# A two-layer trunk on one core: the state-space stage without GpSimd arithmetic, and the first fetched rows moved in the first expert stage

## The chip, the cores and the metric

The kernel runs on one core of one Trainium2 chip. Its time is device microseconds (us). Before the change three runs gave 1828.47, 1831.72 and 1833.39 us; the median is 1831.72 us. The profile is of one further execution of 1835.46 us, whose span from the first to the last instruction is 1833.7 us.

The names of the engines in the profile: PE is TensorE's matmul, PEld its weight load, DVE is VectorE, ACT is ScalarE, POOL is GpSimd, SP is SyncE, which here only sends for data. A q behind a name (SPq, POOLq) is that engine's own queue of semaphore waits and DMA issues.

## The reference

256 image tokens and 256 context tokens of 1024 channels go through two layers, all in float32. Layer 0 mixes tokens by attention and by a state-space scan (SSD), layer 1 by two kinds of attention. After each mixer stand a residual with a layer norm and a mixture of 32 experts. What the change touches:

```python
# the state-space branch: a depthwise convolution of 5 taps, then silu
u = jax.nn.silu(depthwise_conv_centred(xbc, conv_w, conv_b))
xs, bm, cm = split(u)                       # 1024 + 512 + 512 channels
# ssd_chunk_scan, per chunk of 128 tokens, 4 groups of 4 heads, two directions
decay = exp(where(lower, a_cs[l] - a_cs[s], -inf))
y_diag = einsum(decay * (cm @ bm.T), x)
y_off  = einsum(cm, h_in, exp(a_cs))
# the experts: each token goes to 2 of 32
x   = layer_norm(ALPHA * x + gate * mix, ln_g[0], ln_b[0])
f   = hier_moe(modulate(x, ...))            # w2[e] (silu(w1[e] x) * (w3[e] x))
out = layer_norm(ALPHA * x + gate5 * f, ln_g[1], ln_b[1])
```

## The kernel before, in words

The work runs in stages: the first modulation and the attention of layer 0 (up to about 240 us of the trace), the state-space scan (240 to 480 us), the output projection, residual and routing (to 580 us), the experts of layer 0 (to about 1095 us), then the same for layer 1. Apart from instructions that the code pins (`mmp`, `trp` and a few more), the order on each engine is set when the program is built, by a scheduler that weighs costs; at run time each engine works its list strictly in that order.

**The state-space scan** (`ssd0`) goes through 4 groups. For each group three units of the input projection are split into a high and a low part (`split`, L99 on ACT and L100 on DVE or POOL: `wh`, `wl`), and PE multiplies in three passes (L105 to L107, `pfm`). `self.lo_pool` says which half of a unit has its low part made on POOL. `ssd_conv` then convolves: ACT copies the projection out of PSUM into a padded buffer (`up`, L643), DVE makes the first tap and the bias with one TENSOR_SCALAR (L646), and the four other taps with SCALAR_TENSOR_TENSOR (L648, `acc`). There are 4 groups of 4 such blocks. `ssd_group` takes the decay rows `bc` from DRAM, per chunk `t`: `ce = exp(bc)` on ACT (L796) times `cT` on POOL (L797; 512 columns for the chunks 0 and 1, 1024 for 2 and 3), the difference of the decays by 4 SCALAR_TENSOR_TENSOR on DVE (L802), and twice the product with the mask `cbm` (L808): direction 1 on POOL, direction 0 on DVE. PE sums the products into `py` (L815).

**The experts of layer 0** (`moe`, `nt == 4`) stream weights: each expert needs 6 transfers of 1 MB (L430), into a ring of 12 buffers. A transfer is issued by SP when PE has used the buffer's last contents. For expert `e`, `expert_up` makes the product with w1 and w3 in two halves (`a`, 16 matmuls each), `expert_turn` turns the gated result of the expert before it (`hp`), `expert_down` multiplies by w2 (`py`). Experts come in groups of 4 that share a gathered input `xg`. The input of group 0 comes by matmul. For group 1 and later, POOL fetches the token rows from DRAM by an indirect DMA (`fetch`, L1126), by a row number that PE and DVE make in `group_gates` (`pgs`, then `ix`, L1125), and PE turns them in four steps (`turn_rows`, 4 transposes each, L201 `pg`). `steps` is the list of such pending pieces, and `fill(n, steps)` does n of them at a place in the loop over experts. Since PE's order is pinned there, all later matmuls stand behind a transpose that waits for its rows.

Between expert 0 and the loop stands the residual's affine part: POOL multiplies the 4 tiles of the residual `S` by `ALPHA * ln_g` and adds `ALPHA * ln_b` (L1043, 16 instructions; ACT scales the rows first, L1041). Its constant `alpha` is made from `odest`, so that it starts after the routing.

Of the kernel before, what the change touches and what calls it, by code (L numbers as in the profile page):

```python
# [24 lines left out]
F32 = mybir.dt.float32  # L25
# [3 lines left out]
AF = mybir.ActivationFunctionType  # L29
OP = mybir.AluOpType  # L30
# [4 lines left out]
ALPHA = 4.0 ** 0.25  # L35
# [32 lines left out]
class Trunk:  # L68
# [5 lines left out]
    def pool(self, name, side="left"):  # L74
# [3 lines left out]
        a="rkb pfm pv pck pgk pcq pgq pmq pmv pmk a13 pna pout1",  # L78
# [249 lines left out]
    def mixer0(self):  # L328
        nc, tc, I = self.nc, self.tc, self.I
# [61 lines left out]
            qk = [self.fm(self.w_in(0), hTh, hTl), self.fm(self.w_in(1), hTh, hTl, "pfm2")]  # L391
        self.late_consts()
        self.attention0(qk, small, hTh, hTl, naT, dtb, ad)
        self.lo_pool = lambda jh: jh % 2
        self.ssd0(small, hTh, hTl, YT, dtb, ad, es_a)
        es_h.close()
        self.moep = self.left.enter_context(self.pool("moe"))
# [236 lines left out]
    def ssd_conv(self, sp, g, hTh, hTl, YT, cw, cb, dsk, ups):  # L634
        nc, I, V = self.nc, self.I, self.nc.vector
        bT = sp.tile([128, 512], F32, name="bT", bufs=2)
        cT = sp.tile([128, 512], F32, name="cT", bufs=2)
        xs = sp.tile([128, 4, 256], F32, name="xs", bufs=2)
        Bt = sp.tile([128, 4, 128], F32, name="Bt", bufs=2)

        def sink(f, p):
            up = ups[f % 2]
            nc.scalar.activation(up[:, :, 2:258], p.rearrange("p (s n) -> p s n", s=2), AF.Copy)  # L643
            acc = sp.tile([128, 2, 256], F32, name="acc", bufs=2)
            k = 4 * g + f
            V.tensor_scalar(acc, up[:, :, 0:256], cw[:, k, 0:1], cb[:, k:k + 1], op0=OP.mult, op1=OP.add)  # L646
            for i in range(1, 5):
                V.scalar_tensor_tensor(acc, up[:, :, i:i + 256], cw[:, k, i:i + 1], acc, op0=OP.mult, op1=OP.add)  # L648
            th = sp.tile([128, 2, 256], F32, name="th", bufs=1)
            nc.scalar.activation(th, acc, AF.Tanh)  # L650
            dst = th if f < 2 else (bT if f == 2 else cT).rearrange("p (s n) -> p s n", s=2)
            V.scalar_tensor_tensor(dst, th, 1.0, acc, op0=OP.add, op1=OP.mult)
            if f < 2:
                dfl = dst.rearrange("p s n -> p (s n)")
                nc.scalar.activation(YT[:, 2 * g + f, :], dfl, AF.Copy, scale=dsk[:, 2 * g + f:2 * g + f + 1])
            if f < 3:
                dfl = dfl if f < 2 else bT
                pt = self.ps([128, 4, 128], "xsT")
                for t in range(4):
                    self.tr(pt[:, t], dfl[:, t * 128:(t + 1) * 128])  # L660
                nc.scalar.activation(xs[:, :, f * 128:(f + 1) * 128] if f < 2 else Bt, pt, AF.Copy)

        for u in range(2):
            self.proj_fm(self.w_in(6 + 2 * g + u), hTh, hTl, lambda f, p, u=u: sink(2 * u + f, p))
        return bT, cT, xs, Bt
# [80 lines left out]
    def ssd_group(self, sp, g, bT, cT, xs, Bt, YT, masks, dd):  # L746
# [40 lines left out]
        for t in range(4):  # L787
            sl = slice(t * 128, (t + 1) * 128)
            bc = sp.tile([128, 2, 4, 128], F32, name="bc", bufs=3)
            src = atd[t, :, 4 * g:4 * g + 4, :]  # L790
            nc.sync.dma_start(bc, bass.AP(tensor=src.tensor, offset=src.offset,
                                          ap=[[0, 128], [2048, 2], [128, 4], [1, 128]]))
            dirs = {0: (1,), 1: (0,), 2: (0, 1), 3: (0, 1)}[t]
            d0, d1 = dirs[0], dirs[-1] + 1
            ce = sp.tile([128, 2, 4, 128], F32, name="ce", bufs=2)
            nc.scalar.activation(ce[:, d0:d1], bc[:, d0:d1], AF.Exp)  # L796
            nc.gpsimd.tensor_tensor(ce[:, d0:d1].rearrange("p d r l -> p (d r) l"), ce[:, d0:d1].rearrange("p d r l -> p (d r) l"),  # L797
                            cT[:, None, sl].to_broadcast([128, 4 * (d1 - d0), 128]), OP.mult)
            for r in range(4):
                h = 4 * g + r  # L800
                nc.scalar.activation(bc[:, 1, r], bc[:, 1, r], AF.Identity, bias=nacs[:, t, 16 + h:17 + h])
                V.scalar_tensor_tensor(bc[:, 0, r], bc[:, 0, r], acs[:, t, h:h + 1], bc[:, 1, r],  # L802
                                       op0=OP.subtract, op1=OP.min)
            nc.scalar.activation(bc[:, 0], bc[:, 0], AF.Exp)

            M = bc
            for d in (1, 0):
                (nc.gpsimd if d else V).tensor_tensor(M[:, d], bc[:, 0],  # L808
                                                      cbm[d][:, t:t + 1, :].to_broadcast([128, 4, 128]), OP.mult)
            for f in range(2):  # L810
                terms = [(xdt[d][:, t, :], M[:, d]) for d in range(2)] + [(hst[d][t][:, 0], ce[:, d]) for d in dirs]
                for i, (l, m) in enumerate(terms):
                    for s in range(2):
                        r = 2 * f + s
                        nc.tensor.matmul(py[f][64 * s:64 * s + 64, t, :], l[:, r * 64:(r + 1) * 64], m[:, r],  # L815
                                         start=(i == 0), stop=(i == len(terms) - 1))
# [171 lines left out]
    def moe(self, layer, tiles):  # L988
# [4 lines left out]
        with ExitStack() as es:  # L993
            with self.pool("exp", "right") as ep:
# [5 lines left out]
                def fill(n, q=todo):  # L1000
                    for _ in range(min(n, len(q))):
                        q.pop(0)()
# [27 lines left out]
                fill(2, steps)  # L1030
                self.expert_up(cur, 0, 1)
                self.route_rest(nt)

                alpha = ep.tile([128, 1], F32, name="alpha")
                V.tensor_scalar(alpha, self.odest[:, nt - 1, 1:2], 0.0, ALPHA, op0=OP.mult, op1=OP.add)
                for h in range(2):
                    k = slice(512 * h, 512 * h + 512)
                    for n, y, op in (('ln_g', "yh", OP.mult), ('ln_b', "yl", OP.add)):
                        a = ep.tile([128, 512], F32, name=y, bufs=3)
                        nc.gpsimd.dma_start(a, self.bcast(I[n][layer, 0, k], 512))  # L1040
                        nc.scalar.activation(a, a, AF.Copy, scale=alpha)  # L1041
                        for t in tiles:
                            G.tensor_tensor(S[:, t, k], S[:, t, k], a, op)  # L1043
                self.dump(f'L{layer}_dest', self.dest)
                self.dump(f'L{layer}_gate', self.gate)
                prev = None
# [4 lines left out]
                for e in range(nb + 1):  # L1051
# [5 lines left out]
                    if cur and e:  # L1057
                        self.expert_up(cur, 0)
                    fill(2)
                    fill(2 if e > 28 or nt == 4 and e % 4 == 1 else 1, steps)  # L1060
                    if prev:
                        self.expert_turn(prev)
                    if cur:
# [17 lines left out]
                    if e == 0:  # L1081
                        group(1)
                        fill(2 if nt == 2 else 1, steps)
                    if e % 4 == 3 and e < 27:
                        group(e // 4 + 2)
                    if e == 27:
# [78 lines left out]
    def group_gates(self, ep, nt, oh, e, rows=None):  # L1165

        gs = ep.tile([64, 4], F32, name="gs", bufs=3)
        for i in range(2):
# [2 lines left out]
                self.mmp(pg.rearrange("p a b -> p (a b)"), oh[:, t, 128 * i:128 * i + 128], self.gdr[:, t].rearrange("p a b -> p (a b)"),  # L1171
                         start=(t == 0), stop=(t == nt - 1))
            if rows is not None:
                self.fetch(ep, rows[:, i], pg[:, 0, 32:33])
            for k in range(2):
                self.nc.vector.tensor_reduce(gs[:, 2 * i + k:2 * i + k + 1], pg[64 * k:64 * k + 64, :, e + 2 * i + k], AX.X, OP.add)
        return gs
# [770 lines left out]
```

## Time and profile before

| what | value |
|---|---|
| runs (us) | 1828.47, 1831.72, 1833.39; median 1831.72 |
| profiled execution (us) | 1835.46, span 1833.7 |
| PE, DVE, ACT, POOL busy (us) | 1680.1, 968.9, 507.8, 374.6 |
| mean granted TensorE clock | 0.953 of full speed |
| DMA | 536.16 MB, mean 292 GB/s |

The busy times are averages over stages that differ: in the two expert stages the DMA engines are busy all the time at 420 GB/s, and in the stages between them at a half or less. A stage has to be read on its own.

### The profile page before, as it was taken

What the parts mean: (1) busy time and instruction counts of PE and PEld (TensorE: products, weight loads), DVE (VectorE), ACT (ScalarE), POOL (GpSimd) and SP (SyncE); (2) the same over time, 40 slices, a digit from 0 to 9 for tenths busy, and PEclk for the clock granted to TensorE, in tenths of its full rate; (3) what the DMA queues carried; (4) which work ended last, traced back from release to release, by engine and by line L of the source; (5) the groups of instructions that cost most, each with busy time, mean ns of one, the idle gap of its engine ahead of it and who ended that gap; (6) DMA issues with size and microseconds to landing.
All of it is one profiled execution on the core that took longest, in us unless ns stands there. A gap on an engine that the chain in (4) does not pass through costs nothing. (4 is left out here: it accounts for less than half of the span.)

```text
span 1833.7 us, 21779 instructions
## 1 busy us (share of the span) xinstructions
PE 1680.1 (92%) x8093; PEld 871.2 (48%) x8093; DVE 968.9 (53%) x2025; ACT 507.8 (28%) x987; POOL 374.6 (20%) x313
## 2 busy tenths in 40 slices
PE   7999989999898799999999995989979999999995
PEld 2665646557455343444443333856444444444441
DVE  2454469878667155544554447774553333433325
ACT  2423434434122111111111113467321111111111
POOL 2211114433122322121211114331020000100101
PEclk8999999999998899999999996989989999999997
DMA  9665265654626799999999971253369999999993
GB/s 340 212 205 186 77 227 172 223 197 114 235 76 241 310 419 420 421 421 420 421 421 420 413 325 62 79 218 114 123 256 421 421 421 421 421 420 421 421 420 143
DMA packets 103072, 536.16 MB, mean 292 GB/s; under 512 B 20657, under 2 KB 24753, under 8 KB 49329
## 3 DMA queue, kind: packets, MB, share of 16 engines
q1 hardware_dynamic: 98032, 519.69, 71.9%
q0 software_dynamic: 4928, 15.02, 2.3%
q8 instruction: 66, 1.08, 0.2%
q14 instruction: 46, 0.37, 0.1%
HBM read 531.36 MB, written 3.30 MB: 292 GB/s over the span
## 5 line engine op out<-in xcount | busy, mean ns | idle before, releaser
L197 PE MATMUL a<-ringw,xg 128*64 128x512 f32 x1584 | 371.4, 611 | 0.8 <-DVE ovbase L1833 0.5
L197 PEld LDWEIGHTS a<-ringw,xg 128*64 128x64 f32 x1584 | 114.4, 141 | 212.8 <-issue 205.7
L1196 DVE TENSOR_TENSOR ym<-pcm,mod 128x512 f32<-128x512 f32 x136 | 90.6, 688 | 168.5 <-PE pcm L197 167.5
L1773 DVE TENSOR_TENSOR yl<-py,yh 64x512 fp32r<-64x512 f32 x130 | 89.5, 688 | 162.5 <-ACT yh L1772 162.4
L1197 POOL TENSOR_TENSOR S<-S,ym 128x512 f32<-128x512 f32 x68 | 86.5, 1272 | 403.7 <-DVE ym L1196 403.7
L1772 ACT ACTIVATE yh<-py 64x512 fp32r<-64x512 f32 x130 | 76.9, 591 | 275.1 <-PE py L197 224.3
L197 PE MATMUL py<-ringw,g 128*64 128x512 f32 x640 | 146.0, 597 | 0.0
L1197 POOL TENSOR_TENSOR S<-S,two 128x512 f32<-128x512 f32 x32 | 40.9, 1278 | 410.3 <-DVE two L1196 410.3
L197 PE MATMUL a<-raw,xg 128*64 128x512 f32 x496 | 116.2, 607 | 1.8 <-DMA raw<-in_moe_w_dram 1.8
L105 PE MATMUL pfm<-hTh,wh 128*128 128x512 f32 x256 | 107.5, 421 | 8.5 <-ACT up L643 5.8
L216 PE MATMUL adaps<-adw,cs 128*32 128x512 f32 x384 | 97.6, 656 | 13.5 <-DMA adw<-in_ada_w_dram 13.4
L100 POOL TENSOR_TENSOR wl<-raw,wh 128x512 fp32r<-128x512 f32 (+1 forms) x46 | 58.7, 1281 | 237.2 <-ACT wh L99 148.0
L106 PE MATMUL pfm<-hTh,wl 128*128 128x512 f32 x256 | 104.5, 408 | 0.0
L107 PE MATMUL pfm<-hTl,wh 128*128 128x512 f32 x256 | 101.5, 403 | 0.0
L1747 ACT ACTIVATE sa<-a 64x512 f32<-64x512 f32 x65 | 38.4, 591 | 217.0 <-PE a L197 217.0
L197 PE MATMUL pcm<-yh,ohT 128*128 128x512 f32 (+1 forms) x200 | 91.6, 458 | 6.6 <-DVE ym L1196 4.5
L1196 DVE TENSOR_TENSOR two<-pcm,S 128x512 f32<-128x512 f32 x64 | 42.7, 689 | 94.7 <-PE pcm L197 94.2
L197 PE MATMUL py<-raw,g 128*64 128x512 f32 x400 | 91.3, 598 | 0.5 <-ACT g L1756 0.5
L197 PEld LDWEIGHTS py<-ringw,g 128*64 128x64 f32 x640 | 43.8, 136 | 81.1 <-issue 74.1
L197 PE MATMUL pcm<-yl,ohT 128*128 128x512 f32 (+1 forms) x200 | 81.1, 406 | 0.6 <-DVE yl L1773 0.6
L197 PEld LDWEIGHTS pcm<-yh,ohT 128*128 128x128 f32 (+1 forms) x200 | 38.2, 191 | 91.4 <-issue 64.8
L1748 DVE SCALAR_TENSOR_TENSOR sa<-sa,gs,a 64x512 f32<-64x512 f32 x64 | 47.9, 749 | 52.0 <-ACT sa L1747 50.6
(519 smaller groups left out, 2872.8 us busy)
## 6 DMA issues: line engine op xcount, KB each, us to landing
ringw<-in_moe_w_dram SPq DMA_DIRECT2D x278, 1024.0 KB, 16.5
raw<-in_moe_w_dram SPq DMA_DIRECT2D x112, 1024.0 KB, 15.2
adw<-in_ada_w_dram SPq DMA_DIRECT2D x96, 512.0 KB, 5.2
raw<-in_w_in_dram SPq DMA_DIRECT2D x18, 1024.0 KB, 6.9
bc<-atd SPq DMA_DIRECT2D x16, 512.0 KB, 6.6
raw<-in_w_out_dram SPq DMA_DIRECT2D x4, 1024.0 KB, 5.9
raw<-in_o_w_out_dram SPq DMA_DIRECT2D x4, 1024.0 KB, 4.8
bias<-in_rpb_dram SPq DMA_DIRECT2D x8, 256.0 KB, 4.8
```

Of the source, the lines that this page charges most:

```text
L100: (eng or nc.vector).tensor_tensor(lo, src, hi, OP.subtract)
L105: mm(out, ah, bh, start=start, stop=False)
L106: mm(out, al, bh, start=False, stop=False)
L107: mm(out, ah, bl, start=False, stop=stop)
L197: return self.tc.keep_in_program_order(self.nc.tensor.matmul(*args, **kw))
L216: self.nc.tensor.matmul(p[32 * g:32 * g + 32, :], self.cs[:, j, :], w[:, (g - g0) * 512:(g - g0 + 1) * 512], start=(j == 0), stop=(j == 7))
L1196: nc.vector.tensor_tensor(m, p, self.rows5[t // 2][:, k], OP.mult)
L1197: (nc.gpsimd if i % 2 == 0 else nc.vector).tensor_tensor(S[:, t, k], S[:, t, k], m, OP.add)
L1747: self.nc.scalar.activation(s, a[0:64, :], AF.Silu)
L1748: self.nc.vector.scalar_tensor_tensor(s, s, E['gs'], a[64:128, :], op0=OP.mult, op1=OP.mult)
L1772: nc.scalar.activation(c[h][0][r], py[q], AF.Copy)
L1773: V.tensor_tensor(c[h][1][r], py[q], c[h][0][r], OP.subtract)
```

## The change

Four edits of the state-space stage and two of the expert stage:

1. `lo_pool` is False there: all low parts `wl` of the stage's projections are made on DVE.
2. The middle tap and the bias are made by ACT, straight from PSUM (ACTIVATE Identity with scale and bias); DVE adds the other four taps. The TENSOR_SCALAR is gone.
3. `ce` times `cT` is on DVE.
4. Both products with `cbm` are on DVE.
5. The affine part of layer 0 is issued after the fetch of group 1's rows, and `alpha` is made from that fetch's row number; for layer 1 (`nt == 2`) it stays.
6. The turning of group 1's rows, formerly two steps at expert 1 and one each at experts 2 and 3, is now two at expert 2 and two at expert 3.

```diff
-        self.lo_pool = lambda jh: jh % 2
+        self.lo_pool = lambda jh: False
...
-            nc.scalar.activation(up[:, :, 2:258], p.rearrange("p (s n) -> p s n", s=2), AF.Copy)
...
-            V.tensor_scalar(acc, up[:, :, 0:256], cw[:, k, 0:1], cb[:, k:k + 1], op0=OP.mult, op1=OP.add)
-            for i in range(1, 5):
+            pv = p.rearrange("p (s n) -> p s n", s=2)
+            nc.scalar.activation(up[:, :, 2:258], pv, AF.Copy)
+
+            nc.scalar.activation(acc, pv, AF.Identity, scale=cw[:, k, 2:3], bias=cb[:, k:k + 1])
+            for i in (0, 1, 3, 4):
                 V.scalar_tensor_tensor(acc, up[:, :, i:i + 256], cw[:, k, i:i + 1], acc, op0=OP.mult, op1=OP.add)
...
-            nc.gpsimd.tensor_tensor(ce[:, d0:d1].rearrange("p d r l -> p (d r) l"), ce[:, d0:d1].rearrange("p d r l -> p (d r) l"),
+            V.tensor_tensor(ce[:, d0:d1].rearrange("p d r l -> p (d r) l"), ce[:, d0:d1].rearrange("p d r l -> p (d r) l"),
...
-                (nc.gpsimd if d else V).tensor_tensor(M[:, d], bc[:, 0],
+                V.tensor_tensor(M[:, d], bc[:, 0],
...
+                if nt == 2:
+                    affine(self.odest[:, nt - 1, 1:2])
...
-                    fill(2 if e > 28 or nt == 4 and e % 4 == 1 else 1, steps)
+
+                    fill({1: 0, 2: 2, 3: 2}.get(e, 2 if e > 28 or e % 4 == 1 else 1) if nt == 4 else 2 if e > 28 else 1, steps)
...
                         fill(2 if nt == 2 else 1, steps)
+                        if nt == 4:
+                            affine(self.number)
...
-                self.fetch(ep, rows[:, i], pg[:, 0, 32:33])
+                self.number = pg[:, 0, 32:33]
+                self.fetch(ep, rows[:, i], self.number)
```

POOL at the start of the expert stage, before (`rows` are the fetched rows, `S` the residual, `yh` and `yl` the scaled rows of ln_g and ln_b):

```order
L1040 DMA yl<-in_ln_b_dram 128x512
L1043 TENSOR_TENSOR S<-S,yh 128x512 x4
L1126 DMA rows<-h2d,ix 128x1024
L1043 TENSOR_TENSOR S<-S,yh 128x512 x2
L1043 TENSOR_TENSOR S<-S,yl 128x512
L1043 TENSOR_TENSOR S<-S,yh 128x512 x2
L1126 DMA rows<-h2d,ix 128x1024
L1043 TENSOR_TENSOR S<-S,yl 128x512 x7
```

And the same place of the changed program (L1126 has become L1135, L1043 is L1046):

```order
L1043 DMA yl<-in_ln_b_dram 128x512
L1135 DMA rows<-h2d,ix 128x1024 x2
L1046 TENSOR_TENSOR S<-S,yh 128x512 x7
L1046 TENSOR_TENSOR S<-S,yl 128x512
L1046 TENSOR_TENSOR S<-S,yh 128x512
L1046 TENSOR_TENSOR S<-S,yl 128x512 x7
```

Both fetches now stand ahead of all 16 affine instructions, where the second one stood behind nine. PE in the same place, before, from the row numbers (`pgs`) on:

```order
L197 MATMUL pgs<-gdr,two_4502 128x66 x8
L197 MATMUL a_4540<-ringw,xg 64x512 x8
L201 MATMUL pg<-ident,rows 128x128 x8
L201 MATMUL hp<-ident,sa 128x64 x4
L197 MATMUL a_4540<-raw,xg 64x512 x8
L201 MATMUL poT<-ident,two_4180 128x128 x4
```

And of the changed program:

```order
L197 MATMUL pgs<-gdr,two_4472 128x66 x8
L197 MATMUL a_4540<-ringw,xg 64x512 x8
L201 MATMUL hp<-ident,sa 128x64 x4
L197 MATMUL a_4540<-raw,xg 64x512 x8
L201 MATMUL poT<-ident,two_4180 128x128 x4
L197 MATMUL py_4582<-raw,g 64x512 x8
L197 MATMUL a_4603<-ringw,xg 64x512 x8
L201 MATMUL pg<-ident,rows 128x128 x8
L201 MATMUL hp<-ident,sa 128x64 x4
```

The first eight transposes of the rows have moved behind the rest of expert 1 and the first half of expert 2. The last chunks of the last group on DVE, before (`cb` are the masked products, `YT` the result):

```order
L784 TENSOR_TENSOR h_3505<-h_3505,pst 128x256
L802 SCALAR_TENSOR_TENSOR bc<-bc,acs 128x128 x8
L808 TENSOR_TENSOR bc<-bc,cb_3467 128x512 x2
L819 TENSOR_TENSOR YT<-YT,py 128x512
L679 SCALAR_TENSOR_TENSOR YT<-zt,YT 128x512
```

And of the changed program:

```order
L786 TENSOR_TENSOR h_3505<-h_3505,pst 128x256
L799 TENSOR_TENSOR ce<-ce,cT 128x1024
L804 SCALAR_TENSOR_TENSOR bc<-bc,acs 128x128 x4
L799 TENSOR_TENSOR ce<-ce,cT 128x1024
L804 SCALAR_TENSOR_TENSOR bc<-bc,acs 128x128 x2
L810 TENSOR_TENSOR bc<-bc,cb_3468 128x512
L804 SCALAR_TENSOR_TENSOR bc<-bc,acs 128x128 x2
L810 TENSOR_TENSOR bc<-bc,cb_3467 128x512
L810 TENSOR_TENSOR bc<-bc,cb_3468 128x512
L810 TENSOR_TENSOR bc<-bc,cb_3467 128x512
L821 TENSOR_TENSOR YT<-YT,py 128x512
```

What POOL did for these two chunks (two `ce`, two products) now stands in DVE's own list, between its other work.

## Rows read from the trace of the kernel before

**Rows 1.** Busy time by stage: stretch, length, engines' busy us, clock, DMA share, GB/s
```profile
240.00:480.00 240.00, 219.85 (x1226) 145.81 (x1228) 195.39 (x293) 99.00 (x195) 88.81 (x62) 0.94 0.54 175
...
598.90:617.10 18.20, 7.49 (x31) 3.53 (x30) 0.69 (x1) 0.98 (x2) 13.94 (x12) 0.72 0.48 176
617.10:1075.00 457.90, 440.84 (x2024) 185.32 (x2026) 225.06 (x385) 82.54 (x151) 86.78 (x70) 0.98 1.01 418
```

**Rows 2.** The same in 10 us slices, one slice of the state-space stage
```profile
330.00:340.00 10.00, 9.28 (x36) 5.99 (x36) 10.00 (x17) 4.42 (x7) 4.09 (x1) 0.83 0.60 214
```

**Rows 3.** POOL's groups, 240 to 480 us: count, busy us, mean ns, idle before
```profile
L808 POOL TENSOR_TENSOR bc<-bc,cb 128x512 f32<-128x512 f32 x16 | 28.4, 1781 | 19.3 <-issue 7.2 <-ACT bc L804 6.6 <-DVE cb L762 5.4
L100 POOL TENSOR_TENSOR wl<-raw,wh 128x512 fp32r<-128x512 f32 x16 | 21.9, 1370 | 82.5 <-ACT wh L99 41.2 <-DVE acc L648 29.6 <-issue 11.0
L797 POOL TENSOR_TENSOR ce<-ce,cT 128x1024 f32<-128x1024 f32 x8 | 19.1, 2396 | 23.4 <-ACT ce L796 23.4
L797 POOL TENSOR_TENSOR ce<-ce,cT 128x512 f32<-128x512 f32 x8 | 12.2, 1525 | 28.2 <-DVE cT L652 13.0 <-ACT ce L796 5.6 <-ACT bc L801 4.4
```

**Rows 4.** DVE's groups, 240 to 480 us
```profile
L648 DVE SCALAR_TENSOR_TENSOR acc<-up,cw,acc 128x512 f32<-128x512 f32 x56 | 49.4, 890 | 0.5
L802 DVE SCALAR_TENSOR_TENSOR bc<-bc,acs 128x128 f32<-128x128 f32 x64 | 48.1, 787 | 5.8 <-ACT bc L801 5.8
L646 DVE TENSOR_SCALAR acc<-up,cw,cb 128x512 f32<-128x512 f32 x14 | 12.5, 896 | 2.9 <-ACT up L643 2.6
```

**Rows 5.** Single lines on DVE: ns shortest/median/longest, first and last start
```profile
L802 DVE SCALAR_TENSOR_TENSOR bc<-bc,acs x64: 335/345/3331, 244.1 to 476.7; 128x128 f32<-128x128 f32 x64
...
L648 DVE SCALAR_TENSOR_TENSOR acc<-up,cw,acc x56: 734/745/1878, 244.9 to 431.0; 128x512 f32<-128x512 f32 x56
...
L646 DVE TENSOR_SCALAR acc<-up,cw,cb x14: 530/547/1601, 243.7 to 421.6; 128x512 f32<-128x512 f32 x14
...
L808 DVE TENSOR_TENSOR bc<-bc,cb x16: 672/680/1754, 282.0 to 479.1; 128x512 f32<-128x512 f32 x16
...
L767 DVE TENSOR_TENSOR xdt<-xs,dt x8: 1210/1219/2320, 260.4 to 439.6; 128x1024 f32<-128x1024 f32 x8
```

**Rows 6.** Order of time, POOL and DVE at 300 us: start us, us
```profile
300.29 2.41 POOL L797 TENSOR_TENSOR ce<-ce,cT 128x1024 f32<-128x1024 f32 x1
...
300.65 2.20 DVE L802 SCALAR_TENSOR_TENSOR bc<-bc,acs 128x128 f32<-128x128 f32 x1
```

**Rows 7.** Order of time, DVE at the end of the state-space stage
```profile
469.06 4.99 DVE L802 SCALAR_TENSOR_TENSOR bc<-bc,acs 128x128 f32<-128x128 f32 x4 [0.81 <-ACT bc L801]
```

**Rows 8.** Order of time, TensorE at experts 0 and 1 [idle before]
```profile
593.11 5.80 PE L197 MATMUL a<-ringw,xg 128*64 128x512 f32 x16
601.67 0.38 PE L201 MATMUL pg<-ident,rows 128*128 128x128 f32 x1 [2.76 <-DMA rows<-h2d,ix]
610.00 1.76 PE L201 MATMUL pg<-ident,rows 128*128 128x128 f32 x7 [7.95 <-DMA rows<-h2d,ix]
```

**Rows 9.** Order of time, DVE: the row numbers
```profile
591.61 0.16 DVE L1125 CAST ix<-pgs 128x1 int32<-128x1 f32 x1 [0.54 <-PE pgs L197]
...
593.22 0.16 DVE L1125 CAST ix<-pgs 128x1 int32<-128x1 f32 x1 [1.22 <-PE pgs L197]
```

**Rows 10.** Order of time, POOL: the two fetches
```profile
596.03 1.05 POOL L1126 DMA_INDIRECT rows<-h2d,ix  x1 [0.16 <-issue]
...
603.41 1.01 POOL L1126 DMA_INDIRECT rows<-h2d,ix  x1 [0.16 <-issue]
```

**Rows 11.** Order of time, SP: weight transfers of 1 MB
```profile
598.94 0.81 SPq L430 DMA_DIRECT2D ringw<-in_moe_w_dram  x2
617.10 4.51 SPq L430 DMA_DIRECT2D raw<-in_moe_w_dram  x4
```

**Rows 12.** An ACT group with a scale per partition, 240 to 480 us
```profile
L655 ACT ACTIVATE YT<-th,dsk 128x512 f32<-128x512 f32 x8 | 5.7, 716 | 4.6 <-DVE th L652 4.6
```

**Rows 13.** One line of the expert stages on DVE: ns shortest/median/longest
```profile
L1748 DVE SCALAR_TENSOR_TENSOR sa<-sa,gs,a x64: 743/749/751, 589.2 to 1801.7; 64x512 f32<-64x512 f32 x64
```

More of the change, by code (lines that the diff above doesn't have):

```diff
@@ L1032, in moe, with affine @@
                 self.route_rest(nt)
[L1034 to L1043, printed above, removed]
+                def affine(after):
+                    alpha = ep.tile([128, 1], F32, name="alpha")
+                    V.tensor_scalar(alpha, after, 0.0, ALPHA, op0=OP.mult, op1=OP.add)
+                    for h in range(2):
+                        k = slice(512 * h, 512 * h + 512)
+                        for n, y, op in (('ln_g', "yh", OP.mult), ('ln_b', "yl", OP.add)):
+                            a = ep.tile([128, 512], F32, name=y, bufs=3)
+                            nc.gpsimd.dma_start(a, self.bcast(I[n][layer, 0, k], 512))
+                            nc.scalar.activation(a, a, AF.Copy, scale=alpha)
+                            for t in tiles:
+                                G.tensor_tensor(S[:, t, k], S[:, t, k], a, op)
+                if nt == 2:
+                    affine(self.odest[:, nt - 1, 1:2])
                 self.dump(f'L{layer}_dest', self.dest)
```

## The prediction

> **What bounds the kernel now.** I read first the busy times by stage, then the stage's busiest groups, then single lines of code, then the order of time where something stalls. The stages differ [rows 1]. From 617.10 to 1075 us the DMA engines are busy all the time at 418 GB/s: there the weights of the experts set the pace, a transfer lost at the start is lost at the end, and a stage that begins earlier ends earlier by as much. Ahead of that stand two stages in which DMA is half idle, and both are changed.
>
> In the state-space stage (240 to 480 us) TensorE is busy for 219.85 of 240 us at a mean granted clock of 0.94, and VectorE for 195.39 [rows 1]. The mean hides that VectorE has slices without a gap, in which TensorE idles and its clock falls: from 330 to 340 us VectorE is busy 10.00 of 10 us, and the clock is 0.83 [rows 2]. So here VectorE's list sets the end for much of the stage, and TensorE only a little behind it. GpSimd works beside it on the low parts, the masked products and `ce`: 28.4 + 21.9 + 19.1 + 12.2 = 81.6 us [rows 3].
>
> The second thing to see is that VectorE's times are not all its own. L802 has a mean of 787 ns and a median of 345, L648 890 and 745, L646 896 and 547, and the longest of L802 takes 3331 ns [rows 4, 5]. The order of time shows what happens: GpSimd's `ce` runs from 300.29 for 2.41 us, and an L802 that starts beside it at 300.65 takes 2.20 us and ends as `ce` ends [rows 6]. At the end of the stage four L802, which at the median would take 1.4 us, take 4.99 [rows 7]. I take mean minus median as what GpSimd costs VectorE.
>
> At the start of the expert stage TensorE stops twice at the transposes of the fetched rows, for 2.76 and 7.95 us [rows 8]. The row numbers were ready at 591.61 and 593.22 us [rows 9], but GpSimd sent for the rows at 596.03 and 603.41 [rows 10], since affine instructions stood ahead of the fetches in its list. While TensorE stops no buffer comes free: SP issues two transfers at 598.94 and the next at 617.10 [rows 11], and DMA moves 176 GB/s in between [rows 1].
>
> **The change part by part.** *Edits 1, 3 and 4 (GpSimd's work to VectorE).* Added to VectorE in the stage: 16 low parts and 16 products, each 128x512 TENSOR_TENSOR; their price is the median of the same operation there, 680 ns [rows 5], so 32 x 0.680 = 21.8 us. The `ce` of 512 columns cost 8 x 0.680 = 5.4 us, those of 1024 columns 8 x 1.219 = 9.8 us at the median of L767, which is as wide [rows 5]. Sum 37.0 us. (The low parts made before 240 us go to a stage that I leave at zero: VectorE is not near full there, and they only run ahead of TensorE.) Taken away: the stretch, 64 x (787 - 345) = 28.3 us at L802, 56 x (890 - 745) = 8.1 at L648, 14 x (896 - 547) = 4.9 at L646 [rows 4, 5]; sum 41.3 us. Smaller groups stretch too; I leave them out.
>
> *Edit 2 (the middle tap on ScalarE).* VectorE loses 14 TENSOR_SCALAR in the stage at 547 ns, 7.7 us [rows 5]. ScalarE gains 14 ACTIVATE with a scale per partition; the nearest row is L655, 716 ns [rows 12], so 10.0 us on an engine busy 99.00 of 240 us [rows 1]. Behind the new instruction on ScalarE's list stand the next copy out of PSUM and the decays' exponentials; they come at most 0.72 us later per block, which I cost at nothing because VectorE, which takes them, is the later of the two. If that cover is gone, each of 14 blocks is longer by 716 - 547 ns, 2.4 us in all.
>
> VectorE's list thus changes by 37.0 - 7.7 - 41.3 = -12.0 us. How much of it reaches the end? From above: TensorE cannot gain more than its idle time, 240 - 219.85 = 20.2 us, and what the half clock costs, 0.06 x 219.85 = 13.2 us, together 33 us [rows 1]. From below: if the stretch stayed, VectorE would have 29.3 us more work. I take 12 us, the list's own change, because the slices without a gap are where TensorE stops, and the small groups left out stand against those parts of the stage where VectorE is not full. The end of the stage points the same way: the four L802 of 4.99 us shrink by about 3.6, and two `ce` at 2.396 us become 1.219 each, though now in VectorE's own list.
>
> The Trainium skill (SBUF — State Buffer, section "Who interferes with whom") says that a VectorE instruction with two inputs in SBUF and a GpSimd instruction that reads SBUF exclude each other, and that the one that comes second waits for the whole of the first. L802 and L648 have two inputs in SBUF, and the pair at 300 us agrees. By the rule GpSimd would also be the one that waits, and the shared port would be the resource to count; that is the second rival below.
>
> *Edits 5 and 6 (fetch first, turn later).* With the fetches ahead of the affine part, POOL sends for the rows at about 592 and 594 us instead of 596.03 and 603.41 [rows 9, 10]. In the old list the rows landed 5.6 and 6.6 us after the issue (601.67 - 596.03, 610.00 - 603.41) [rows 8, 10], so they would land by 601 us. And TensorE does not ask for them until expert 2, when it has done the rest of expert 1 and half of the next one. Both waits go: 2.76 + 7.95 = 10.7 us [rows 8]. The 16 transposes remain, only elsewhere. For DMA the gain is the time in which it moved less than its rate: 18.2 x (418 - 176) / 418 = 10.5 us [rows 1]. The two agree, and I take 10.5. What is late next is DMA itself, from 604 us on. The affine part starts a few microseconds later, but without the two fetches of 1.05 and 1.01 us between its instructions [rows 10]; POOL's next work, the sums of the first two experts, needs products that TensorE has not begun, so I cost the shift at nothing, and at those few microseconds of POOL's time, not TensorE's, if that cover is gone. The added wait is `alpha`'s, for the second row number; behind it on ScalarE stands the next expert's copy out of PSUM, which needs TensorE's transposes after 599 us and so loses nothing. Bounds: at most the 10.7 us; at least 7.95 if the first rows still held TensorE.
>
> Sum: 12.0 + 10.5 = 22.5 us. The profiled execution took 1835.46 us, so the changed one would take 1813.0; against the median of the runs, 1831.72, it is 1809.2, and I predict 1809.
>
> **The rivals.** *Only the expert stage gains.* TensorE is busy 92% of the state-space stage, and each group's chain goes through ScalarE, VectorE and TensorE in turn; with less stretch but a longer list of its own VectorE may deliver no sooner. Against it stand the slices without a gap and the clock. 1831.7 - 10.5 = 1821.
>
> *The port is the bound.* Then VectorE's two-input work and GpSimd's run one after the other, and what counts is that 81.6 us of GpSimd leave the port while 37.0 come back [rows 3], a fall of 44.6 and with the taps 52 us: more than TensorE can show, so that the stage gains the whole 33 us: 1831.7 - 33 - 10.5 = 1788. Against it: VectorE and GpSimd are busy 195.39 + 88.81 = 284 us in 240 [rows 1], so for 44 us at least they did run side by side. The rule behind this rival is the one of the Trainium skill's page on SBUF that is named above.
>
> *VectorE becomes the bound (slower).* If the long L802 waited for something other than GpSimd, the stretch stays and VectorE's list of 195.4 us grows by 37.0 - 7.7 = 29.3 us with no second engine to take a share: 1831.7 + 29.3 - 10.5 = 1850. It decides the sign as soon as less than 18.8 of the 41.3 us of stretch goes away. Against it: the pair of rows at 300 us that end together.
>
> *The expert stage does not gain.* The affine part now runs beside expert 1, and its 16 instructions could hold up VectorE's gating `sa`, for which TensorE waits. That would have shown already, since POOL adds to the residual all through the stage, and `sa` takes 743 to 751 ns [rows 13]. Or TensorE, 440.84 of 457.9 us busy [rows 1], had the slack to make the stop good later; but DMA had none. 1831.7 - 12 = 1820.
>
> **How the numbers follow.** The forecast 0.60, its own range 1801 to 1817; only the expert stage 0.17; the port 0.12; no gain at the experts 0.07; slower 0.04. The range 1796 to 1822 leaves out most of the port's case, a part of the two cases at 1820, and the slow one, about 0.2 together. About 0.3%, 5.5 us, is what a measurement of this kernel can tell from no change. Faster by more, below 1826.2 us: 0.60 + 0.12 + most of 0.17 and 0.07 = 0.93; within it 0.03; slower 0.04.
>
> **What would show it.** In the profile of the changed kernel L802, L648 should have means at their medians, 345 and 745 ns, and none over 1 us; VectorE's busy time in the state-space stage about 12 us less; GpSimd none; the mean clock there above 0.94. TensorE should have no wait for `rows` at experts 0 to 3, and SP's transfers no gap between 599 and 617 us (shifted by the earlier stage's gain). I am wrong if L802 stays stretched, if TensorE's waits for VectorE in the state-space stage grow, or if the stretch of DMA at full rate begins less than 15 us earlier.

## The result, and the profile after

The changed kernel takes 1799.53 us (median of 4 runs, 1798.8 to 1802.7) against 1830.1 us of the kernel before (median of 4). The ratio is 0.9836, with a 95% interval from 0.9822 to 0.9851: 30 us, faster. The forecast was 1809 us. Its two mechanisms hold; the gain of the state-space stage is larger than its term, 12.0 us.

The profiled execution has a span of 1797.9 us, 35.8 less than that of before; its mean granted clock is 0.966 (before 0.953). The end of the last `py` of the scan moves from 481.8 to 462.8 us (-19.0), the first expert matmul from 579.58 to 561.81 (-17.8). The first transfer of layer 1's weights, which marks the end of the first expert stage, moves from 1077.03 to 1047.06 (-30.0), so that the experts give 12.2. The 5.8 us that are left lie in layer 1, where nothing was changed and the order on every engine is the same. About half of it comes from a collision of GpSimd and VectorE that the last section shows, and about half from one product at the end, for which TensorE took 6.01 us in the profile of before (at 1794.18 us) and 3.65 in that of the changed kernel: in the 10 us around it the granted clock is 0.66 of full speed before, and 1.00 after.

One profile is one execution, and that of before stood 5.4 us above the median of its runs. The experiments e2, e3 and e4 below leave the state-space stage as it was, in the same order on every engine. From the start of its first tap to its last `py` it took 252.5 us in the profile of before and 246.5, 249.1 and 249.5 in theirs. The changed stage took 232.2 us, and 232.6 in e1, which has it in the same order. So the stage's gain is 14 to 20 us, and the -19.0 stands near the upper end. With the expert stage as before, e1 needs 496.5 us for it, before 497.5; with both expert edits it is 485.3 in the changed kernel and 484.5 in e2: 11 to 13 us.

The windows of the changed kernel: start and end, us, then busy us and count of PE, PEld, DVE, ACT and POOL, the clock, the DMA share and GB/s. The first answers to the first of [rows 1], but begins at 230 us, where the stage's first blocks do:

```profile
230.00:463.00 233.00, 220.10 (x1298) 148.39 (x1298) 183.59 (x341) 110.88 (x216) 7.81 (x14) 0.99 0.61 187
572.00:581.10 9.10, 6.21 (x28) 3.21 (x26) 3.57 (x20) 4.07 (x6) 3.35 (x4) 0.82 1.02 428
581.10:586.60 5.50, 5.50 (x28) 1.97 (x26) 0.00 (x0) 0.74 (x2) 5.50 (x5) 0.99 1.04 405
586.60:1045.00 458.40, 441.31 (x2038) 186.05 (x2036) 225.66 (x386) 83.13 (x152) 99.59 (x81) 0.99 1.01 420
```

The same view of the kernel before, over the same work (1299 matmul rows against 1298):

```profile
230.00:482.00 252.00, 228.53 (x1299) 150.24 (x1298) 201.95 (x304) 100.68 (x198) 89.36 (x62) 0.94 0.55 180
```

VectorE does 37 instructions more and is busy 18.4 us less; the stage is 19 us shorter. What GpSimd still does there is three MEMSETs and DMA issues, no arithmetic. On TensorE, 23.5 us of idle time became 12.9, and the same matmuls take 8.4 us less, at a granted clock of 0.99 instead of 0.94. The hole of [rows 1], 598.90 to 617.10 us, moved by the 17.8 us of the stages ahead, would lie at 581.10 to 599.30. DMA moves 405 and 420 GB/s there, where it moved 176: the hole is gone. It runs at its rate without a break from 572 us on, where it did so from 617.10.

Single lines of the changed kernel (nanoseconds: shortest, median and longest): the decay differences, the taps on VectorE and the tap on ScalarE. They answer to [rows 5, 12]:

```profile
L804 DVE SCALAR_TENSOR_TENSOR bc<-bc,acs x64: 338/346/353, 238.0 to 456.4; 128x128 f32<-128x128 f32 x64
L650 DVE SCALAR_TENSOR_TENSOR acc<-up,cw,acc x64: 735/745/753, 231.4 to 414.7; 128x512 f32<-128x512 f32 x64
L648 ACT ACTIVATE acc<-pfm,cb,cw x16: 757/770/785, 230.6 to 406.8; 128x512 f32<-128x512 f32 x16
```

No decay difference is longer than 353 ns, where one took 3331: the whole stretch is gone. The order of time on VectorE at the stage's end shows the four that took 4.99 us in [rows 7]:

```profile
452.87 1.14 DVE L804 SCALAR_TENSOR_TENSOR bc<-bc,acs 128x128 f32<-128x128 f32 x4
```

The start of the experts, changed kernel, order of time, POOL then SP then PE, answering to [rows 8, 10, 11]:

```profile
577.42 1.05 POOL L1135 DMA_INDIRECT rows<-h2d,ix  x1 [13.85 <-DVE gs L1186]
578.77 0.98 POOL L1135 DMA_INDIRECT rows<-h2d,ix  x1 [0.30 <-DVE ix L1134]
...
583.37 0.81 SPq L430 DMA_DIRECT2D ringw<-in_moe_w_dram  x2
587.58 4.51 SPq L430 DMA_DIRECT2D raw<-in_moe_w_dram  x4
595.18 12.96 SPq L430 DMA_DIRECT2D ringw<-in_moe_w_dram  x8
...
595.09 1.16 PE L201 MATMUL pg<-ident,rows 128*128 128x128 f32 x8
608.75 1.31 PE L201 MATMUL pg<-ident,rows 128*128 128x128 f32 x8 [0.32 <-DVE ym L1206]
```

The two fetches follow each other, the transposes find their rows (no `DMA rows` as releaser), and SP's hole of 18.2 us has become steps of 4.2 and 7.6 us.

Something that the prediction did not look at: in the kernel before, TensorE stopped at the very start of the scan. Order of time, kernel before, ACT and PE:

```profile
241.67 0.63 ACT L796 ACTIVATE ce<-bc 128x512 f32<-128x512 f32 x1 [7.20 <-DMA bc<-atd]
242.21 0.61 ACT L650 ACTIVATE th<-acc 128x512 f32<-128x512 f32 x1
242.73 0.58 ACT L643 ACTIVATE up<-pfm 128x512 f32<-128x512 f32 x1
...
243.36 0.80 PE L105 MATMUL pfm<-hTh,wh 128*128 128x512 f32 x1 [5.82 <-ACT up L643]
```

The copy out of PSUM stood in ScalarE's list behind a `ce` whose decay rows were still on their way, and TensorE waited 5.82 us for that copy. In the changed kernel this stop is absent.

### The profile page after: what moved, and what is told of

Its sections match the earlier page's. It is cut to its first block, busy times and chain, and to the rows that moved or that the text cites. A ratio compares the mean times of both kernels' runs of the same rounds, so it can differ in the third digit from the quotient of the medians.

```text
span 1797.9 us, 21742 instructions
## 1 busy us (share of the span) xinstructions
PE 1662.9 (92%) x8093; PEld 861.7 (48%) x8093; DVE 949.2 (53%) x2065; ACT 517.1 (29%) x1003; POOL 284.0 (16%) x257
## 5 line engine op out<-in xcount | busy, mean ns | idle before, releaser
L216 PE MATMUL adaps<-adw,cs 128*32 128x512 f32 x384 | 96.2, 643 | 14.9 <-DMA adw<-in_ada_w_dram 14.9
L1207 DVE TENSOR_TENSOR S<-S,ym 128x512 f32<-128x512 f32 x68 | 66.5, 978 | 1.8
## 6 DMA issues: line engine op xcount, KB each, us to landing
raw<-in_moe_w_dram SPq DMA_DIRECT2D x112, 1024.0 KB, 18.4
```

The source lines that it names most:

```text
L216: self.nc.tensor.matmul(p[32 * g:32 * g + 32, :], self.cs[:, j, :], w[:, (g - g0) * 512:(g - g0 + 1) * 512], start=(j == 0), stop=(j == 7))
L1207: (nc.gpsimd if i % 2 == 0 else nc.vector).tensor_tensor(S[:, t, k], S[:, t, k], m, OP.add)
```

## The experiments

The end of the last `py` matmul of each of the four groups of the scan, us, tells where in the stage an edit acts. It is read from the order of time of each kernel:

| kernel | group 1 | 2 | 3 | 4 | group 4 alone | runs, median us |
|---|---|---|---|---|---|---|
| before | 314.6 | 375.8 | 438.7 | 481.8 | 43.1 | 1830.1 |
| changed | 300.1 | 363.9 | 416.8 | 462.8 | 46.0 | 1799.53 |
| e6, idle reads | 309.4 | 380.7 | 453.0 | 502.4 | 49.4 | 1839.14 |
| e7, idle memsets | 297.8 | 361.6 | 414.1 | 466.1 | 52.0 | 1803.38 |
| e8, columns by GpSimd | 297.2 | 361.0 | 414.2 | 458.2 | 44.0 | 1796.35 |
| e9, low parts back | 309.8 | 360.2 | 410.4 | 466.8 | 56.4 | 1806.82 |
| e10, `ce` back | 299.5 | 364.0 | 413.4 | 477.7 | 64.3 | 1814.41 |
| e11, products back | 303.4 | 356.4 | 410.3 | 463.9 | 53.6 | 1803.32 |
| e12, e10 and e8 | 299.0 | 363.6 | 415.1 | 475.2 | 60.1 | 1811.22 |

Two cautions for all of them. The scheduler sets a new order with most edits, and in this table TensorE's and ScalarE's lists are the same only in e8 and the changed kernel, and in e10 and e12, which agree on VectorE too. So one undone edit is not the only thing that differs. And the experiments ran at other times than the changed kernel: the kernel before took 1826.83 to 1831.03 us (medians) beside them, so that a few us between two rows are not settled by the times. By the ratios to the kernel before, e5 stands 5 us above the changed kernel, e7 7, e9 10, e10 17, e11 6 and e12 8.

The diffs below show the lines that decide, with `...` for what is left out; the remarks behind `#` are no part of the code.

### e1: edits 1 to 4 alone, and e2: edits 5 and 6 alone

```diff
+        self.lo_pool = lambda jh: False        # e1: with edits 2, 3, 4
...
+                        if nt == 4:
+                            affine(self.number)  # e2: with edit 6
```

> The four edits of the state-space stage alone (low parts, products and ce on VectorE, middle tap on ScalarE); the expert stage as before. If the two places add up, the scan stage ends about 19 us earlier (as in the changed kernel's trace) and the time is about 1830 - 18 = 1812 us, with TensorE still stopped about 10 us for the fetched rows. If the gain of the scan stage is partly given back where the expert stage begins, it is 1818 or more.

> The two edits of the expert stage alone; the scan as before. If the 10.7 us of TensorE's stop are what is gained, 1830 - 11 = 1819 us, and the scan stage keeps its long L802 instructions. If the affine part, now beside expert 1, holds up VectorE, less: 1825 us.

e1 took 1809.41 us, ratio 0.9889 [0.9869, 0.991]: 20 us. e2 took 1818.17 us, 0.995 [0.9931, 0.997]: 9 us. Within their intervals the two add up to the whole, so the halves are independent as far as this can tell. In e1's trace the scan ends at 462.4 us as in the changed kernel, and TensorE's waits for rows are back (10.8 us); in e2's the stage from the first expert matmul to the first transfer of layer 1 takes 484.5 us, against 497.5 of before. The rivals "only the expert stage gains" and "the expert stage does not gain" fall.

### e3: fetch first alone, and e4: turn later alone

```diff
+                        if nt == 4:
+                            affine(self.number)                    # e3: edit 5
...
+                    fill({1: 0, 2: 2, 3: 2}.get(e, ...) ..., steps)  # e4: edit 6
```

> The fetch ahead of the affine part, but turned at expert 1 as before. If the late fetch is the cause and rows take 5.6 to 6.6 us as before, TensorE waits under 2 us for them: 1830 - 9 = 1821 us. If the rows take the median of 9.5 us, it waits about 5 us: 1825 us. If the place of the turning is what counts, nothing is gained: 1830 us.

> The turning at experts 2 and 3, but the fetches between the affine instructions as before. The second fetch lands about 610 us in the old trace, and TensorE comes to the turning at about 611 us if it is not stopped before: then nothing waits, 1819 us, as with both edits. If the fetch must also go first, because the rows land later beside running weight transfers, a wait of 3 to 8 us stays: 1822 to 1827 us.

e3 took 1824.11 us, 0.9973 [0.9963, 0.9983]; e4 1821.6, 0.996 [0.9946, 0.9974]: 5 and 7 us. The expert stage is 7.9 us shorter in e3 and 10.5 in e4, against 12.2 with both (all against the profile of before). PE in the order of time, e3:

```profile
600.85 0.38 PE L201 MATMUL pg<-ident,rows 128*128 128x128 f32 x1 [1.32 <-DMA rows<-h2d,ix]
602.05 1.04 PE L201 MATMUL pg<-ident,rows 128*128 128x128 f32 x7 [0.82 <-DMA rows<-h2d,ix]
```

and e4:

```profile
609.39 0.38 PE L201 MATMUL pg<-ident,rows 128*128 128x128 f32 x1
611.40 1.04 PE L201 MATMUL pg<-ident,rows 128*128 128x128 f32 x7 [1.63 <-DMA rows<-h2d,ix]
```

Each edit alone takes most of the 10.7 us of [rows 8] away and leaves a stop of 2.1 or 1.6 us. They are two cures of one wait; their gains must not be added. The rows took 7.7 us and more from issue to landing in e3, which is why fetching them first did not suffice alone.

### e5: the middle tap back on VectorE

```diff
+            nc.scalar.activation(up[:, :, 2:258], p.rearrange("p (s n) -> p s n", s=2), AF.Copy)
+            V.tensor_scalar(acc, up[:, :, 0:256], cw[:, k, 0:1], cb[:, k:k + 1], op0=OP.mult, op1=OP.add)
+            for i in range(1, 5):
```

> The changed kernel with the convolution's first tap back on VectorE (TENSOR_SCALAR) in place of the middle tap on ScalarE. If VectorE's list sets the end of the scan stage throughout, it is longer by 16 x 0.547 = 8.8 us: 1808 us. If ScalarE's additional step (16 x 0.77 us, for which VectorE waited 15.5 us) costs as much as it saves, no change: 1800 us.

It took 1802.56 us, 0.9862 [0.9843, 0.9881]; the interval overlaps that of the changed kernel at its edge. The scan ends at 462.85 us against 462.83, with VectorE busy for 185.63 us against 183.59. With GpSimd out of the way VectorE has room for the tap: the trace shows no gain of edit 2, and by the times it is worth a few us at most. The tap that is back has lost its stretch, [rows 5] had 1601 ns for its longest:

```profile
L646 DVE TENSOR_SCALAR acc<-up,cw,cb x16: 535/541/547, 227.8 to 408.8; 128x512 f32<-128x512 f32 x16
```

So GpSimd also stretched a line with one tensor input. In the profile of before, all six of its instructions over 1 us overlap a `ce`, a product or a low part of GpSimd's and end 0.3 us after one; that writes alone do not stretch it, no run shows.

### e6: idle reads, and e7: idle memsets

Both add unused work to the changed kernel: GpSimd writes a slice of `YT` that is overwritten later, in groups 0 to 2, with two inputs read from SBUF (e6, 48 instructions) or none (e7, 120).

```diff
+            if g < 3:
+                first = nc.gpsimd.tensor_copy(YT[:, 7, 0:1], hst[dirs[0]][t][:, 0, 0:1])
+                with self.tc.issue_after(first.ins):
+                    for _ in range(4):
+                        nc.gpsimd.tensor_tensor(YT[:, 7], bT, cT, OP.mult)   # e7: range(10), memset(YT[:, 7], 1.0)
```

> The changed kernel with 48 more GpSimd TENSOR_TENSOR of 128x512 in groups 0 to 2 of the scan stage, which read two SBUF tiles and whose result nothing uses: 61 us of GpSimd, nothing added to VectorE. If GpSimd's reads are what stretched VectorE, L804, L650 and the other VectorE instructions with two SBUF inputs are stretched to over 1 us again, and the time grows by 10 to 30 us: 1810 to 1830 us. If the long instructions came from waiting for GpSimd's results, nothing is stretched and the time stays 1800 us.

> The same as with the added reads, but 120 GpSimd MEMSETs of 128x512 (about 64 us), which read nothing. If only a GpSimd instruction that reads SBUF holds VectorE up, no VectorE instruction is stretched and the time is 1800 us. If any GpSimd instruction does, it is as slow as with the added reads.

e6 took 1839.14 us, 1.0058 [1.0039, 1.0077], 40 us above the changed kernel; e7 1803.38, 0.9873 [0.9853, 0.9893], 4 us above it. Single lines of e6 (L805 is the idle read, L809 the decay difference, L650 the taps):

```profile
L805 POOL TENSOR_TENSOR YT<-bT,cT x48: 1262/1299/2332, 283.4 to 443.6; 128x512 f32<-128x512 f32 x48
L809 DVE SCALAR_TENSOR_TENSOR bc<-bc,acs x64: 334/346/1710, 238.1 to 495.0; 128x128 f32<-128x128 f32 x64
L650 DVE SCALAR_TENSOR_TENSOR acc<-up,cw,acc x64: 735/744/1851, 232.3 to 451.9; 128x512 f32<-128x512 f32 x64
```

Its stage, in the columns of the windows above:

```profile
230.00:502.00 272.00, 233.42 (x1298) 156.94 (x1298) 227.15 (x340) 112.07 (x216) 86.02 (x74) 0.92 0.52 160
```

and of e7:

```profile
L805 POOL MEMSET YT<- x120: 525/527/547, 281.5 to 417.4; 128x512 f32 x120
L809 DVE SCALAR_TENSOR_TENSOR bc<-bc,acs x64: 333/344/354, 236.0 to 459.6; 128x128 f32<-128x128 f32 x64
```

with its stage:

```profile
230.00:466.00 236.00, 221.68 (x1289) 148.79 (x1288) 183.53 (x341) 109.10 (x214) 77.94 (x146) 0.97 0.62 183
```

GpSimd is busy 86.0 and 77.9 us. Beside reads VectorE's list grows by 43.6 us (227.15 - 183.59), and the stage by 39.6; beside memsets it stays as it was. The 3.3 us by which e7's scan ends later arise in group 4, behind the memsets, where TensorE stops once for an instruction that stands behind a late router column in VectorE's list:

```profile
PE pst L780 <- DVE xdec L774: 6.2, 1, 6.2
```

The lists of e6 and e7 differ from each other in some 20 places on TensorE and on VectorE, so that the 36 us between their times come from the reads rather than from the order. A stretch of VectorE's list thus reaches the end at some nine tenths, with TensorE's clock down to 0.92. e6 in the order of time:

```profile
298.92 6.99 POOL L805 TENSOR_TENSOR YT<-bT,cT 128x512 f32<-128x512 f32 x4
...
301.07 1.24 DVE L246 TENSOR_TENSOR lnsh<-modc,lncol 128x16 f32<-128x16 f32 x1
```

Even a VectorE instruction of 16 columns (166 ns in the changed kernel) takes 1.24 us beside a read: it waits, however short it is. The Trainium skill (SBUF — State Buffer, section "Who interferes with whom") says that a two-input VectorE instruction collides with a GpSimd instruction that reads SBUF, and not with one that only writes it. e6 and e7 agree, 1710 against 354 ns for the longest decay difference.

### e8: the router's columns sent for by GpSimd

```diff
-            nc.sync.dma_start(col, self.prow[layer, s].rearrange("m (j p) -> p m j", p=128))
+            (nc.sync if layer else nc.gpsimd).dma_start(col, self.prow[layer, s].rearrange("m (j p) -> p m j", p=128))
```

> The changed kernel with the two loads of the router's columns (rcol) of layer 0 issued by GpSimd, which is idle there, in place of SP. In the changed kernel VectorE waited 5.8 us for them at the end of the scan stage, and TensorE was idle for 3.75 us between 450 and 460 us. If those loads stand late because of SP's list, 3 to 5 us are gained: 1796 us. If GpSimd needs longer for 2048 elements of 4 bytes than SP, nothing, or a loss: 1800 to 1805 us.

It took 1796.35 us, 0.983 [0.9812, 0.9847], the lowest median of all; the interval overlaps that of the changed kernel, so the 3 us are not settled by the times. Nor does the trace settle them: with TensorE's list the same, group 4 ends 4.6 us earlier, but groups 1 to 3, where the columns play no part, already end 2.6 to 2.9 us earlier. Group 4 alone is 2.0 us shorter, and between the changed kernel and e1, in the same order, it differs by 1.0. VectorE's waits, changed kernel (us, times, longest):

```profile
DVE wrs L922 <- DMA rcol<-prow: 5.8, 2, 3.3
```

and e8:

```profile
DVE wrs L922 <- DMA wr<-in_router_dram: 3.9, 1, 3.9
```

The columns are no longer late; the router's weights now are.

### e9, e10, e11: one piece each back on GpSimd

```diff
+        self.lo_pool = lambda jh: jh % 2                               # e9
...
+            nc.gpsimd.tensor_tensor(ce[:, d0:d1]...                    # e10
...
+                (nc.gpsimd if d else V).tensor_tensor(M[:, d], bc[:, 0],   # e11
```

> The changed kernel with edit 1 undone: every second low part of a weight block is made by GpSimd again (8 before 240 us and 16 behind it). Open is where the part of the state-space gain comes from that the list of VectorE does not hold: in the profile of before TensorE stops 5.8 us at 237.5 us, at the start of the stage, for ScalarE's copy out of PSUM, which stands behind a decay that waits for its broadcast; in the changed kernel that stop is gone. Theory (edit 1 takes the stop away, since it changes when weight buffers come free and in which order the first blocks are made): the stop comes back, and the list of VectorE changes by little (16 x 0.68 = 10.9 us less, against a stretch of 41.3 x 21.9 / 81.6 = 11.1 us): 5 to 7 us slower than the changed kernel, about 1806. Rival (the stop went for another edit): no stop, within 2 us of the changed kernel, about 1800. Port as the bound: 21.9 us come to the port and 10.9 go: 11 us slower, 1811.

> The changed kernel with edit 3 undone: the 16 products of the decay with C (`ce`) run on GpSimd again, 31.3 us of its time in the trace of before. Theory (VectorE's own list counts, and GpSimd stretches it in proportion to its busy time): 15.2 us leave VectorE's list and 41.3 x 31.3 / 81.6 = 15.8 us of stretch come back: the same to 3 us slower, 1800 to 1803. Rival (the port is the bound): 31.3 - 15.2 = 16 us slower, 1816. In its trace the decay differences (128x128) beside a `ce` should take up to 2.5 us under both.

> The changed kernel with edit 4 undone: 16 of the 32 masked products run on GpSimd again, 28.4 us of its time in the trace of before. Theory (VectorE's list): 16 x 0.68 = 10.9 us leave it and 41.3 x 28.4 / 81.6 = 14.4 us of stretch come back: 3 to 5 us slower, 1803 to 1805. Rival (the port is the bound): 28.4 - 10.9 = 17.5 us slower, 1817. Third reading: TensorE takes the product at the end of each group's chain, so that a slower one (1.78 against 0.68 us) is waited for 16 times: up to 16 x 1.1 = 17.6 us slower too, but then TensorE's wait for the product is the largest of the stage and VectorE's decay differences keep their 345 ns for the most part.

e9 took 1806.82 us, 0.989 [0.9869, 0.9911]; e10 1814.41, 0.993 [0.9903, 0.9957]; e11 1803.32, 0.9867 [0.9848, 0.9887]: 7, 15 and 4 us above the changed kernel. The sizes of e9 and e11 fit the theory, but not its reasons. In e9 the stop at the stage's start does not come back; TensorE has a new wait for GpSimd, but in group 1:

```profile
PE pfm L106 <- POOL wl L100: 4.7, 1, 4.7
```

At the end of group 3 both are ahead of the changed kernel, by 6.4 and 6.5 us. They lose it in group 4, in which TensorE stops for a product `yt` (e9, then e11):

```profile
PE pna L940 <- DVE yt L942: 6.1, 1, 6.1
PE pna L940 <- DVE yt L942: 5.5, 1, 5.5
```

In VectorE's list this `yt` stands behind a wait for the router's columns, as in e10 below; in the changed kernel the same stop takes 1.2 us. These two runs therefore price the order of the last group above all, and not the stretch.

e10 fits the port in size and not in place. Up to the end of group 3 it is level with the changed kernel (413.4 against 416.8), which a port that is full all the time would not allow. It loses 15 us in group 4. VectorE and PE there, e10, order of time:

```profile
449.46 4.99 DVE L804 SCALAR_TENSOR_TENSOR bc<-bc,acs 128x128 f32<-128x128 f32 x4 [0.34 <-ACT bc L803]
...
463.45 0.46 DVE L922 TENSOR_TENSOR wrs<-wr,rcol 128x288 f32<-128x288 f32 x1 [6.14 <-DMA rcol<-prow]
...
467.49 0.68 DVE L942 TENSOR_TENSOR yt<-pna,r_gate 128x512 f32<-128x512 f32 x1
...
468.22 5.81 PE L940 MATMUL pna<-raw,two 128*128 128x512 f32 x8 [12.02 <-DVE yt L942]
```

The stretched differences are back (4.99 us), VectorE then waits 6.14 us for a router column, and TensorE waits 12.02 us for a product behind both.

### e12: `ce` on GpSimd, with the columns of e8

> The kernel with `ce` back on GpSimd (1814.41 us against the changed kernel's 1799.53), and the router's two column loads issued by GpSimd instead of SP, as in the run that took 1796.35. Open is why `ce` costs 15 us where the list of VectorE gives 0 to 3. Theory (order at the stage's end): in the trace with `ce` back VectorE waits 8.2 us for `rcol` in order, with the last four decay differences and products behind the second wait, and TensorE stops 12.0 us until 468 us; when the columns come earlier most of that goes: 1800 to 1804, 3 to 7 us above the run with the columns alone, and no wait of TensorE over 6 us at the stage's end. Rival (stretch and the port over the whole stage): the 15 us stay, 1808 to 1812, with the wait gone or not.

It took 1811.22 us, 0.988 [0.9855, 0.9905], 3 us below e10 with the same lists on PE, DVE and ACT. The column's wait is gone, and TensorE's stop is halved:

```profile
PE pna L940 <- DVE yt L942: 6.3, 1, 6.3
```

But the scan still ends 12.4 us after that of the changed kernel, where e10's ends 14.9 after it, and the time lies in the rival's range. So the router's column is at most a small part of e10's loss; the stretch at the end (4.76 us for the four differences) and the new order of group 4 are left, and how they share the rest stays open.

## Why the prediction was right, and where its size was off

*VectorE's stretch comes from GpSimd's work, and goes with it.* Right: 41.3 us were put on three lines, and their means are now the medians. e6 makes the stretch again with idle reads, e7 shows that a busy GpSimd alone doesn't. The slower rival, in which the stretch stays, falls with it.

*VectorE's list changes by -12.0 us.* This is the term that was mis-sized: by busy time it measures -18.4. "Smaller groups stretch too; I leave them out" was worth 6.1: `xdt` 1.5, `xdec` of 768 columns 1.1, `th` 1.0, `h` 0.7, the products that were on VectorE before 1.0 (747 to 684 ns) and its own low parts 0.8 (734 to 684 ns). Each added instruction cost what was reckoned, but 20 low parts instead of 16 came into the stretch, which took 2.8 us of that back. The rest lies in how it is measured: the durations of VectorE's records, which the sum was made of, fall by 15.1 us, from 220.8 to 205.7. Busy time counts once the moments in which two records overlap, 18.9 us with 304 instructions and 22.1 with 341, and so shows 3.2 us more.

*The list's change is taken in full for the stage.* Right for the two large changes: -18.4 us of list and -19.0 of stage (14 to 20 over the traces), +43.6 and +39.6 in e6. It is no rule for small ones: e10's list is 5.9 us longer than the changed kernel's (189.47 us busy) and its scan ends 14.9 later, e5's is 2.0 longer and ends at the same time. TensorE shows the stage's gain as 10.6 us less idle and 8.4 of clock given back. That list and stage agree so well has some luck in it, since 5.8 of the 10.6 are the stop at the start of the stage, which the prediction did not see, as it left the stretch before 240 us at zero. Which edit removed that stop stays open: no run with one edit undone has it at that length (1.2 us remain in e5), while e2, without the four edits, does (5.5 us).

*The tap costs nothing.* Right; the tap measures 770 ns instead of 716, and e5 shows no clear gain from it either.

*The experts gain 10.5 us.* Right in mechanism; the stage gains 12.2, and the hole of 18.2 us is gone. One step of it did not hold: the rows were to land 5.6 and 6.6 us after their issue, and took 8.7 to 12.3 us in the changed kernel. It cost nothing, since TensorE asks for them only at 595.09 us; with edit 5 alone, in e3, it leaves the stop of 2.1 us. *The affine part hides.* Right for TensorE; VectorE meets GpSimd's sums once, for 1.50 us at 594.58 us, as the last of them held a `yl` buffer.

*The port as the bound.* Its 33 us did not come. The mechanism is real, as e6 shows, but between 230 and 482 us VectorE and GpSimd were busy for 201.95 + 89.36 us in 252, so they also ran side by side, and the stage gave back VectorE's share of the collision, not the sum.

## What to carry to other kernels

Compare mean and median of VectorE's lines wherever GpSimd works beside it, all groups and not the three largest, and count the difference as work that goes when GpSimd's reads go; beside memsets there is none. What a piece of work costs depends on where it lies and on the order that the scheduler then sets: with `ce` back on GpSimd three groups lost nothing and the last one 15 us. An experiment that undoes one edit prices that order too; idle work added beside nearly the same lists separates better. Two edits that cure one wait are priced together, and a prefetch that an in-order engine must wait for is put ahead of other work in the list that sends for it, or asked for later.

## What was not expected of the hardware

GpSimd suffers from the collision too. The prediction names this only in the rival of the port and prices it nowhere. An idle read of 128x512 takes 1299 ns at the median and 2332 at the longest, and in e6 its four at 298.92 us average 1.75 us. An instruction of 16 columns pays for a whole read, 1.24 us instead of 0.17. Between two of these reads VectorE ends one or two instructions; what decides which engine goes next, no run shows.

The same collision makes part of the 5.8 us in layer 1. There GpSimd multiplies the residual by a row (L1380, in the changed kernel L1390) when that row has landed. Order of time, kernel before:

```profile
1209.06 4.67 POOL L1380 TENSOR_TENSOR S<-S,rsq 128x1024 f32<-128x1024 f32 x2 [16.01 <-DMA rsq<-in_ln_g_dram]
1209.32 2.12 DVE L132 SCALAR_TENSOR_TENSOR rsq_t<-rsq_t 128x2 f32<-128x2 f32 x1
1211.46 2.28 DVE L133 SCALAR_TENSOR_TENSOR rsq_y<-rsq_t,rsq_y 128x2 f32<-128x2 f32 x1
```

And the changed kernel:

```profile
1179.37 0.15 DVE L132 SCALAR_TENSOR_TENSOR rsq_t<-rsq_t 128x2 f32<-128x2 f32 x1
1179.72 0.14 DVE L133 SCALAR_TENSOR_TENSOR rsq_y<-rsq_t,rsq_y 128x2 f32<-128x2 f32 x1
1180.19 5.91 POOL L1390 TENSOR_TENSOR S<-S,rsq 128x1024 f32<-128x1024 f32 x2 [17.14 <-DMA rsq<-in_ln_g_dram]
```

Counted from the first transfer of layer 1's weights, GpSimd begins at 132.0 us before and at 133.1 after, and that is enough to catch two instructions of 2 columns or to miss them. Behind them in VectorE's list stands work that TensorE then waits for, and it falls back by about 3 us. e2, e3 and e4 are caught too, with one instruction of 2 columns each. This part of the gain was not aimed at: against the prediction it is luck. Why the row lands 1.1 us later, counted so, stays open.
